# Later vectors with the seventh row block, turned rows of x one block later each

## The chip, the cores and the metric

The kernel runs on one core of a Trainium2 chip. The metric is the device time of one execution in microseconds (us); it is given as the median of several runs.

## The reference, cut to what matters

The program is one layer of a decoder trunk for 512 positions of 1024 channels, in float32: a mixer (an mLSTM head group beside a convolution group) and a causal ConvFFN, each behind a conditioned norm. The change touches only what feeds the first projection:

```python
cond = jax.nn.silu(c)
mod = cond @ ada_w[l] + ada_b[l]
sh1, sc1, g1, sh2, sc2, g2 = jnp.split(mod[:, None, :], N_MOD, axis=-1)
u = rms_norm(x, mix_pre_g[l]) * (1.0 + sc1) + sh1
proj = u @ w_in[l]
...
a, gt = jnp.split(glu, 2, axis=-1)
y = causal_dwconv(a * jax.nn.sigmoid(gt), cv_dw_w[l], cv_dw_b[l])
```

The two halves of `glu` are columns of `proj`, so they are products of `u` (512 x 1024) with columns of `w_in`. `c` is a vector, so a column of `sc1` or `sh1` is one dot product of `silu(c)` with a column of `ada_w`.

## The kernel before

The 1024 channels are 8 blocks of 128 rows (`KT` = 8, numbered k = 0 to 7), and 512 positions are the width of a tile. A tile is [128 partitions, 512]. The opening, up to line 375, makes the eight blocks of `u` one after the other and at once multiplies each with its weights into eight accumulators (`banks0`, the first four channel blocks of both halves of `glu`). So for each block k the opening needs:

- `w_glu0[k]`, the weights of that block for the eight accumulators: one transfer of 512 KB into a tile of the pool `adas`, which has two buffers (line 321).
- `adaT[k]`, the rows of `ada_w` for shift and scale of that block: two transfers of 512 KB into one tile of the pool `raws`, which also has two buffers (`first_load`, line 225). They are issued one block ahead.
- x, turned so that channels lie on the partitions. Blocks 0 to 3 are turned by TensorE from the untransposed x (`x_turn`); blocks 4 to 7 (`TURNED` = 4) come ready turned from memory, one transfer of 256 KB each into `xr[4]` to `xr[7]` (line 331).

VectorE sums the products of `adaT[k]` with `silu(c)` (`ada_sum`, line 276), which gives shift and scale (`gsk`, lines 334 and 335). Float32 products are made of three passes: each operand is split into a high and a low part, the high part by ScalarE (lines 170, 358, 361), the low part by VectorE (lines 171, 365, 367); `wk` are the split weights and `uh` and `ul` (in the code `hi`, `lo`) the split block of `u`. In blocks 4 to 7 line 354 first scales the turned rows by the norm's factor and the gain. TensorE's products are at line 316 in blocks 0 to 3 (all passes with the high part of `u` before those with the low part) and at lines 188 to 190 from block 4 on (three passes for one accumulator after the other, so that the second matmul of a block needs the low part).

All small vectors (gains, biases, convolution taps) lie side by side in one buffer `vec`. Its first 56 columns (`FIRST`; the bias of `ada_w` and the first gain) come early in a transfer of 28 KB on ScalarE's queue (line 229). The later 592 columns come in one transfer of 296 KB (line 328). Their first reader is `cvw` (line 408), which halves the 248 columns of taps of the 31-wide convolution; it is held on VectorE behind the last `ul` of the opening. The taps themselves (line 731) run on VectorE in the midst of everything up to the end of the attention heads; the short convolutions of the projections are line 462.

What sets the order: TensorE and SyncE run in the order of the source. SyncE issues nearly all transfers of the opening, and an issue that waits for a free buffer holds all that stand behind it. In the opening the other three engines keep the order of the source as well (`in_order`); behind it a planner orders them, by the dependencies and a simulated timeline.

```python
with tile.TileContext(nc, schedule_with_timeline_sim=True) as tc:
    with tc.manual_schedule(engines={mybir.EngineType.SP, mybir.EngineType.PE}):
```

In each block k from 1 on, SyncE thus issues: the weights of block k, the two transfers `adaT[k + 1]`, in block 1 the later vectors, and in blocks 1 to 4 one turned row block for use in block 4, 5, 6 or 7.

Of the kernel before, what the change touches and what calls it, by code (L numbers as in the profile page):

```python
# [52 lines left out]
def decoder_layer(ctx, tc, w_glu0, x, xT, c, adaT, vecs, w_glu, w_qko, w_v0, w_v, w_out, w_up, w_down, out):  # L53
# [75 lines left out]
    def vcol(name, i):  # L129
        a = VEC[name][0] + i  # L130
        return vec[:, a : a + 1]
# [32 lines left out]
    def w_split(src, name, pool=None, tag="w", eng=None):  # L164

        n = src.shape[1]
        pool = pool or wpool
        hi = pool.tile([P, T], F32R, tag=tag, name=f"{name}h")
        lo = pool.tile([P, T], F32R, tag=tag, name=f"{name}l")
        S.activation(hi[:, :n], src, AF.Copy)  # L170
        (eng or G).tensor_tensor(out=lo[:, :n], in0=src, in1=hi[:, :n].bitcast(F32), op=ALU.subtract)  # L171
        return hi, lo
# [8 lines left out]
    def blk(pieces, b):  # L181
        hi, lo = pieces[b // 4]
        a = (b % 4) * P
        return hi[:, a : a + P], lo[:, a : a + P]

    def mm3(ps, a, b, start, stop):

        PE.matmul(ps, a[0], b[0], start=start, stop=False)  # L188
        PE.matmul(ps, a[0], b[1], start=False, stop=False)  # L189
        PE.matmul(ps, a[1], b[0], start=False, stop=stop)  # L190
# [30 lines left out]
    def first_load(k):  # L221

        r = raws.tile([P, 2048], F32, tag="raw", name=f"ada{k}")
        for i in range(2):
            nc.sync.dma_start(r[:, i * D : (i + 1) * D], adaT[k][:, i * D : (i + 1) * D])
        first.append(r)
# [8 lines left out]
    TURNED = KT // 2  # L235
# [36 lines left out]
    def ada_sum(k, i):  # L272
        if i == 0:
            part[k] = small.tile([P, 2], F32, tag="adap", name=f"adap{k}")
        junk = small.tile([P, D], BF16, tag="junk", bufs=1, name=f"junk{k}_{i}")
        V.scalar_tensor_tensor(out=junk, in0=first[k][:, i * D : (i + 1) * D], scalar=1.0, in1=cb, op0=ALU.mult, op1=ALU.mult,
                               accum_out=part[k][:, i : i + 1])
# [6 lines left out]
    def x_out(j, eng):  # L284
        if eng is S:
            S.activation(xr[j], xT_ps[j], AF.Copy)
        else:
            V.tensor_copy(xr[j], xT_ps[j])
# [24 lines left out]
    def passes(wk, k, which):  # L313
        for a, b in ((0, 0), (1, 0), (0, 1)):
            for i in which:
                PE.matmul(banks0[i], blk(wk, i)[a], u[k][b], start=k == 0 and a == b, stop=False)

    for k in range(KT):
        wk = {}
        r = adas.tile([P, D], F32, tag="ada", name=f"wglu0_{k}")  # L320
        nc.sync.dma_start(r, w_glu0[k])
        if k == 0:
            w_hi = wpool.tile([P, T], F32R, tag="w", name="wglu0_0_1h")
            S.activation(w_hi, r[:, T:], AF.Copy)
        if k + 1 < KT:
            first_load(k + 1)
        if k == 1:
            nc.sync.dma_start(vec[:, FIRST:], vecs[:, FIRST:])
        if 1 <= k <= TURNED:
            j = TURNED + k - 1  # L330
            nc.sync.dma_start(xr[j], xT[j - TURNED])
        gsk = small.tile([P, 2], F32, tag="gsk", name=f"gsk{k}")
        gs, sh = gsk[:, :1], gsk[:, 1:]
        V.tensor_scalar(out=gs, in0=part[k][:, :1], scalar1=bp1[:, k : k + 1], scalar2=g32[:, k : k + 1], op0=ALU.add, op1=ALU.mult)
        V.tensor_scalar(out=sh, in0=part[k][:, 1:], scalar1=vcol("ada_b", 2 * k + 1), scalar2=None, op0=ALU.add)
        hi, lo = u[k]
        if k == 0:
            w_lo = wpool.tile([P, T], F32R, tag="w", name="wglu0_0_1l")
            V.tensor_tensor(out=w_lo, in0=r[:, T:], in1=w_hi.bitcast(F32), op=ALU.subtract)
            wk[1] = w_hi, w_lo  # L340
            S.activation(hi, xT_ps[0], AF.Identity, scale=gs, bias=sh)
            S.activation(rb, rb_ps, AF.Copy)
            V.tensor_scalar(out=xr[0], in0=xT_ps[0], scalar1=gs, scalar2=sh, op0=ALU.mult, op1=ALU.add)
            V.tensor_tensor(out=lo, in0=xr[0], in1=hi.bitcast(F32), op=ALU.subtract)
            wk[0] = w_split(r[:, :T], "wglu0_0_0", eng=V)
            for j in range(1, TURNED):
                x_out(j, S)
            for i in range(2):
                ada_sum(1, i)
            passes(wk, k, (6, 7, 4, 5))  # L350
            passes(wk, k, range(4))
            continue
        if k >= TURNED:
            V.scalar_tensor_tensor(out=xr[k], in0=xr[k], scalar=gs, in1=rb, op0=ALU.mult, op1=ALU.mult)
        for b in range(2):
            wk[b] = w_split(r[:, b * T : (b + 1) * T], f"wglu0_{k}_{b}", eng=V)
        if k < TURNED:
            S.activation(hi, xr[k], AF.Identity, scale=gs, bias=sh)
            S.activation(xr[k], xr[k], AF.Identity, scale=gs, bias=sh)
        else:  # L360
            S.activation(hi, xr[k], AF.Identity, bias=sh)
        if k + 1 < KT:
            ada_sum(k + 1, 0)
        if k < TURNED:
            V.tensor_tensor(out=lo, in0=xr[k], in1=hi.bitcast(F32), op=ALU.subtract)
        else:
            last_u = V.scalar_tensor_tensor(out=lo, in0=xr[k], scalar=sh, in1=hi.bitcast(F32), op0=ALU.add, op1=ALU.subtract)
        if k + 1 < KT:
            ada_sum(k + 1, 1)
        if k < 4:  # L370
            passes(wk, k, range(G0))
        else:
            for i, ps in enumerate(banks0):
                mm3(ps, blk(wk, i), u[k], False, k == KT - 1)
# [963 lines left out]
```

## Time and profile before

| What | Value |
| --- | --- |
| Median of three runs | 772.42 us (771.66 to 773.45) |
| The profiled execution's own time | 773.07 us |
| Its span | 771.4 us |
| TensorE (PE) busy, share of the span | 758.4 us, 98% |
| VectorE (DVE) busy | 610.1 us, 79% |
| ScalarE (ACT) busy | 403.8 us, 52% |
| GpSimd (POOL) busy | 352.2 us, 46% |
| Bytes read from and written to memory | 113.22 MB and 11.42 MB |

The profile is of one execution. Its span runs from the first instruction to the last one's end; the profiled execution's own time is 1.67 us longer. PE is TensorE's matmuls and PEld its weight loads, SP is SyncE; a q behind an engine's name (SPq) means that its sequencer issues something. A row of the timeline has the start in us from the span's start, the duration in us, the engine, the line of the kernel, the operation, output and inputs, how many instructions were merged, and in brackets the idle time of the engine before it and what ended it. A row of the chain of waits has start, length and the work or transfer on which the end hung.

### The profile page before, as it was taken

The page shows a single profiled execution, that of the slowest core. Times are in us where ns is not written, and L with a number is a line of the kernel's source. Part 1 is how long each engine was busy: PE and PEld are TensorE (multiplying, and loading weights), DVE is VectorE, ACT ScalarE, POOL GpSimd, SP SyncE. Part 2 cuts the span into 40 slices and gives each one's busy share as a digit, 9 for nine tenths or more (in the row PEclk, how much of TensorE's full clock was granted, in tenths as well). Part 3 has the DMA queues.
Part 4 walks back from the last instruction along what each step waited for, and adds up shares of the span by engine and source line. Part 5 has one row for each costly group of instructions (what it writes and reads, how often), then busy time and mean ns, then how long its engine had stood idle before and what let it go on. Part 6 is the DMA issues. An engine that isn't in the chain of part 4 may idle for free.

```text
span 771.4 us, 10631 instructions
## 1 busy us (share of the span) xinstructions
PE 758.4 (98%) x3709; PEld 637.5 (83%) x3709; DVE 610.1 (79%) x967; ACT 403.8 (52%) x761; POOL 352.2 (46%) x286
## 2 busy tenths in 40 slices
PE   7999999999999999999999999999999999999996
PEld 5788898778888888988888998888888888888885
DVE  6997999999999966756768798666556687799995
ACT  5447266776666447582253555444444444455762
POOL 2029578696798645443661456444444440000001
PEclk9999999999999999999999999999999999999998
DMA  8983214214022452434953753332233321777872
GB/s 320 377 301 132 90 55 164 82 40 151 30 84 107 153 179 105 164 110 164 366 199 126 253 197 130 130 130 88 110 117 129 130 89 62 255 271 241 298 260 109
DMA packets 36409, 125.33 MB, mean 162 GB/s; under 512 B 4194, under 2 KB 5634, under 8 KB 30468
## 3 DMA queue, kind: packets, MB, share of 16 engines
q1 hardware_dynamic: 24372, 96.17, 35.5%
q10 hardware_dynamic: 11984, 28.48, 10.6%
q8 instruction: 29, 0.48, 0.3%
q14 instruction: 24, 0.20, 0.1%
HBM read 113.22 MB, written 11.42 MB: 162 GB/s over the span
## 4 chain that ended last, share of the span: by engine, by line
PE 72%; DVE 21%; DMA 2%; ACT 2%; issue 2%; POOL 0%; ACTq 0%; DVEq 0%; POOLq 0%
PE up L189 10%; PE up L188 10%; DVE cv L731 10%; PE up L190 10%; PE p L1185 4%; PE glu L189 3%; PE glu L190 3%; PE glu L188 3%; PE p L189 3%; PE p L188 3%; PE p L190 3%; PE mixa L188 2%; PE mixa L190 2%; PE mixa L189 2%; PE mixb L189 2%; PE mixb L188 2%
## 5 line engine op out<-in xcount | busy, mean ns | idle before, releaser
L731 DVE SCALAR_TENSOR_TENSOR cv<-gt,cvw,cv 128x505 f32<-128x505 f32 (+24 forms) x200 | 137.3, 729 | 2.3 <-ACT cv L719 1.1
L685 POOL TENSOR_TENSOR ro2r<-ro2t,mhalf 128x1 f32<-128x1 f32 x1 | 0.5, 537 | 119.8 <-DVE ro2t L683 119.8
L727 POOL TENSOR_TENSOR cs<-cs,cs 128x510 f32<-128x510 f32 (+3 forms) x32 | 41.9, 1308 | 0.3
L171 POOL TENSOR_TENSOR wup_1024l<-wup,wup_1024h 128x512 fp32r<-128x512 f32 x20 | 27.4, 1372 | 31.6 <-ACT wup_1024h L170 31.6
L171 POOL TENSOR_TENSOR wup_0l<-wup,wup_0h 128x512 fp32r<-128x512 f32 x20 | 27.7, 1387 | 30.0 <-ACT wup_0h L170 30.0
L171 POOL TENSOR_TENSOR wup_1536l<-wup,wup_1536h 128x512 fp32r<-128x512 f32 x20 | 28.0, 1399 | 27.6 <-ACT wup_1536h L170 25.1
L155 DVE SCALAR_TENSOR_TENSOR junk<-ada,cb 128x1024 bf16<-128x1024 f32 x20 | 31.3, 1565 | 8.5 <-DMA ada<-in_adaT 8.4
L189 PE MATMUL up<-u2l,wup_0h 128*128 128x512 f32 (+1 forms) x100 | 36.5, 365 | 0.2 <-DVE u2l L910 0.2
L188 PE MATMUL up<-u2h,wup_0h 128*128 128x512 f32 (+1 forms) x100 | 36.5, 365 | 0.0
L188 PE MATMUL up<-u2h,wup_1024h 128*128 128x512 f32 (+1 forms) x100 | 36.4, 364 | 0.0
L190 PE MATMUL up<-u2h,wup_0l 128*128 128x512 f32 (+1 forms) x100 | 36.4, 364 | 0.0
L188 PE MATMUL up<-u2h,wup_512h 128*128 128x512 f32 (+1 forms) x100 | 36.4, 364 | 0.0
L189 PE MATMUL up<-u2l,wup_512h 128*128 128x512 f32 (+1 forms) x100 | 36.4, 364 | 0.0
L190 PE MATMUL up<-u2h,wup_512l 128*128 128x512 f32 (+1 forms) x100 | 36.4, 364 | 0.0
L188 PE MATMUL up<-u2h,wup_1536h 128*128 128x512 f32 (+1 forms) x100 | 36.4, 364 | 0.0
L189 PE MATMUL up<-u2l,wup_1536h 128*128 128x512 f32 (+1 forms) x100 | 36.4, 364 | 0.0
L190 PE MATMUL up<-u2h,wup_1536l 128*128 128x512 f32 (+1 forms) x100 | 36.4, 364 | 0.0
L190 PE MATMUL up<-u2h,wup_1024l 128*128 128x512 f32 (+1 forms) x100 | 36.4, 364 | 0.0
L189 PE MATMUL up<-u2l,wup_1024h 128*128 128x512 f32 (+1 forms) x100 | 36.3, 363 | 0.0
L171 POOL TENSOR_TENSOR wup_512l<-wup,wup_512h 128x512 fp32r<-128x512 f32 x20 | 27.7, 1383 | 14.0 <-ACT wup_512h L170 14.0
L725 ACT ACTIVATE cs<-gt,cvw 128x511 f32<-128x511 f32 (+4 forms) x40 | 27.4, 716 | 6.5 <-POOL cs L727 3.2
L170 ACT ACTIVATE wup_1024h<-wup 128x512 fp32r<-128x512 f32 x22 | 13.9, 631 | 25.1 <-PE up L189 20.4
(1072 smaller groups left out, 2667.0 us busy)
## 6 DMA issues: line engine op xcount, KB each, us to landing
wup<-in_w_up SPq DMA_DIRECT2D x22, 1024.0 KB, 6.5
wqko<-in_w_qko SPq DMA_DIRECT2D x12, 1024.0 KB, 4.8
ada<-in_adaT ACTq DMA_DIRECT2D x20, 512.0 KB, 4.6
ada<-in_adaT SPq DMA_DIRECT2D x16, 512.0 KB, 6.9
wo<-in_w_out SPq DMA_DIRECT2D x8, 1024.0 KB, 4.8
spare<-in_adaT ACTq DMA_DIRECT2D x12, 512.0 KB, 7.4
wd<-in_w_down SPq DMA_DIRECT2D x6, 768.0 KB, 6.7
g2kept<-g2d SPq DMA_DIRECT2D x11, 384.0 KB, 7.3
```

The costliest lines, as they stand in the source:

```text
L155: t = V.scalar_tensor_tensor(out=junk, in0=r, scalar=1.0, in1=cb, op0=ALU.mult, op1=ALU.mult, accum_out=mod[:, i : i + 1])
L170: S.activation(hi[:, :n], src, AF.Copy)
L171: (eng or G).tensor_tensor(out=lo[:, :n], in0=src, in1=hi[:, :n].bitcast(F32), op=ALU.subtract)
L188: PE.matmul(ps, a[0], b[0], start=start, stop=False)
L189: PE.matmul(ps, a[0], b[1], start=False, stop=False)
L190: PE.matmul(ps, a[1], b[0], start=False, stop=stop)
L685: G.tensor_tensor(out=r, in0=t, in1=mhalf[:, :1], op=ALU.pow)
L725: S.activation(t[:, d:], cvx[j][:, : T - d], AF.Copy, scale=w(CK - 1 - d))
L727: G.tensor_tensor(out=side[:, d:], in0=side[:, d:], in1=t[:, d:], op=ALU.add)
L731: last_tap[0] = V.scalar_tensor_tensor(out=cp[:, d:], in0=cvx[j][:, : T - d], scalar=w(CK - 1 - d), in1=cp[:, d:], op0=ALU.mult, op1=ALU.add)
L1185: PE.matmul(ps[q], x, y, start=False, stop=m == NM - 1 and i == 2, skip_group_check=True)
```

## The change

The transfer of the later vectors is issued in block 6 instead of block 1, in the same place within the block (behind the two transfers `adaT[k + 1]`). The four turned row blocks are issued in blocks 2 to 5 instead of 1 to 4. The order of SyncE's issues, block by block:

| Block | Before | After |
| --- | --- | --- |
| 1 | w 1, ada 2, vectors, x 4 | w 1, ada 2 |
| 2 | w 2, ada 3, x 5 | w 2, ada 3, x 4 |
| 3 | w 3, ada 4, x 6 | w 3, ada 4, x 5 |
| 4 | w 4, ada 5, x 7 | w 4, ada 5, x 6 |
| 5 | w 5, ada 6 | w 5, ada 6, x 7 |
| 6 | w 6, ada 7 | w 6, ada 7, vectors |
| 7 | w 7 | w 7 |

```diff
         if k + 1 < KT:
             first_load(k + 1)
-        if k == 1:
+        if k == 6:
             nc.sync.dma_start(vec[:, FIRST:], vecs[:, FIRST:])
-        if 1 <= k <= TURNED:
-            j = TURNED + k - 1
+        if 2 <= k <= TURNED + 1:
+            j = TURNED + k - 2
             nc.sync.dma_start(xr[j], xT[j - TURNED])
```

## The prediction

> **What bounds the kernel now.** I read the page first, then the stages of the opening, then the chain of waits, the timeline and the transfers issued by SyncE.
>
> ```profile
> span 771.4 us, 10631 instructions
> PE 758.4 (98%) x3709; PEld 637.5 (83%) x3709; DVE 610.1 (79%) x967; ACT 403.8 (52%) x761; POOL 352.2 (46%) x286
> PE 72%; DVE 21%; DMA 2%; ACT 2%; issue 2%; POOL 0%; ACTq 0%; DVEq 0%; POOLq 0%
> L731 DVE SCALAR_TENSOR_TENSOR cv<-gt,cvw,cv 128x505 f32<-128x505 f32 (+24 forms) x200 | 137.3, 729 | 2.3 <-ACT cv L719 1.1
> ```
>
> TensorE is busy for 98% of the span, so the whole kernel holds only 13.0 us in which it is idle, and DMA is 2% of the chain that ended last. A change of transfers can pay only where a transfer holds TensorE up. The stages show where transfers are dense (columns: busy time of PE, PEld, DVE, ACT and POOL with instruction counts, granted clock, share of the DMA engines, GB/s):
>
> ```profile
> 10.00:20.00 10.00, 9.10 (x50) 8.16 (x50) 8.49 (x18) 5.01 (x11) 1.27 (x2) 1.00 1.01 379
> 20.00:30.00 10.00, 9.95 (x44) 7.94 (x43) 9.40 (x22) 4.50 (x7) 0.00 (x0) 1.00 0.99 375
> 30.00:40.00 10.00, 9.71 (x44) 7.70 (x43) 9.53 (x19) 5.38 (x9) 0.00 (x0) 1.00 1.02 387
> 40.00:50.00 10.00, 10.00 (x46) 8.29 (x45) 10.00 (x20) 3.89 (x7) 0.00 (x0) 1.00 0.90 310
> 120.00:180.00 60.00, 60.00 (x272) 48.34 (x271) 59.65 (x97) 40.39 (x74) 46.10 (x37) 1.00 0.30 105
> ```
>
> From 10 to 40 us the DMA engines are full, at 375 to 387 GB/s; every transfer there delays those queued behind it. TensorE nevertheless runs nearly without a break, at full granted clock. Later, from 120 to 180 us, VectorE is the full engine (59.65 of 60 us). The chain of waits, in order of time, names the one place where the two meet:
>
> ```profile
> 21.83 7.96 DMA wglu<-in_w_glu
> 29.81 0.64 ACT wglu_0h L170
> 30.47 0.69 DVE wglu_0l L171
> 37.97 0.68 DVE ul L367
> 38.70 0.50 PE glu L189
> 116.86 1.28 ACT L574
> ```
>
> The weights of the fourth row block (k = 3), issued at 21.83, land 7.96 us later; ScalarE splits them, VectorE continues, and through VectorE's work of blocks 3 and 4 the chain reaches a matmul at 38.70 us. From there it is TensorE alone, one matmul after the other, up to 116.86 us. So time won at 38.70 is kept at least that far.
>
> ```profile
> 20.39 0.20 DVE L335 TENSOR_SCALAR gsk<-adap,vec 128x1 f32<-128x1 f32 x1
> 29.20 0.20 DVE L335 TENSOR_SCALAR gsk<-adap,vec 128x1 f32<-128x1 f32 x1
> 29.81 0.63 ACT L170 ACTIVATE wglu_0h<-wglu 128x512 fp32r<-128x512 f32 x1 [2.86 <-DMA wglu<-in_w_glu]
> 30.47 0.69 DVE L171 TENSOR_TENSOR wglu_0l<-wglu,wglu_0h 128x512 fp32r<-128x512 f32 x1 [1.07 <-ACT wglu_0h L170]
> 37.90 0.74 DVE L367 SCALAR_TENSOR_TENSOR ul<-xr,gsk,uh 128x512 fp32r<-128x512 f32 x1
> 38.01 0.39 PE L188 MATMUL glu<-uh,wglu_0h 128*128 128x512 f32 x1
> 38.70 0.50 PE L189 MATMUL glu<-ul,wglu_0h 128*128 128x512 f32 x1 [0.29 <-DVE ul L367]
> 39.27 0.39 PE L188 MATMUL glu<-uh,wglu_0h 128*128 128x512 f32 x1
> 43.02 0.75 DVE L367 SCALAR_TENSOR_TENSOR ul<-xr,gsk,uh 128x512 fp32r<-128x512 f32 x1
> 44.04 0.39 PE L188 MATMUL glu<-uh,wglu_0h 128*128 128x512 f32 x1
> ```
>
> VectorE ends its small work for block 3 at 29.40 and stands for 1.07 us, since ScalarE got the weights only at 29.81. In block 4 the first matmul starts at 38.01, the second needs `ul`, which is done at 38.64 (37.90 + 0.74). The stall is larger than the 0.29 us marked as idle. Matmuls 4 (39.27) and 25 (44.04, the first of block 5) are 21 apart, so one takes (44.04 - 39.27) / 21 = 0.227 us; unstalled, matmul 25 would start at 38.01 + 24 x 0.227 = 43.46. It starts 0.58 us later. That is the stall's price.
>
> **The change part by part.**
>
> ```profile
> 15.40 0.43 SPq L328 DMA_DIRECT2D vec<-in_vecs  x1
> 15.87 0.43 SPq L331 DMA_DIRECT2D xr<-in_xT  x1
> 17.91 0.33 SPq L321 DMA_DIRECT2D wglu<-in_w_glu  x1
> 21.18 0.43 SPq L331 DMA_DIRECT2D xr<-in_xT  x1
> 21.83 0.33 SPq L321 DMA_DIRECT2D wglu<-in_w_glu  x1
> 29.98 0.42 SPq L331 DMA_DIRECT2D xr<-in_xT  x1
> 39.81 0.81 SPq L225 DMA_DIRECT2D ada<-in_adaT  x2
> 41.99 0.33 SPq L321 DMA_DIRECT2D wglu<-in_w_glu  x1
> xr<-in_xT SPq DMA_DIRECT2D x4, 256.0 KB, 7.4
> vec<-in_vecs SPq DMA_DIRECT2D x1, 296.0 KB, 6.9
> L354 DVE SCALAR_TENSOR_TENSOR xr<-xr,gsk,rb_s x4: 745/747/750, 34.9 to 50.3; 128x512 f32<-128x512 f32 x4
> L408 DVE TENSOR_SCALAR cvw<-vec x1: 1380/1380/1380, 52.8 to 52.8; 128x248 f32<-128x248 f32 x1
> ```
>
> No instruction and no byte is added or removed; five issues of 0.42 or 0.43 us change places on SyncE's queue. SyncE is not the limit: before 17.91 it has been idle since 16.30, since it waits for a buffer that VectorE frees, so the issues it loses or gains cost nothing.
>
> *Vectors out of block 1, turned rows one block later.* Before, the vectors and the first two turned rows stand ahead of the weights issued at 21.83; after, one turned row does, at about 21.2 us. That is 296 + 256 = 552 KB less ahead, 565,248 bytes, at 375 GB/s 1.51 us. The queue does not run dry meanwhile: time to landing is about 7 us against the 1.51 us taken out. So these weights land near 28.3 us, ScalarE's split ends near 28.9, before VectorE asks for it at 29.40, and the whole 1.07 us goes. The weights issued at 17.91 also land earlier, but VectorE never waited for them. Bounds of this term: 0 (the landing does not move) and 1.07 us (VectorE does not wait, and has its next work queued). I take 1.07, as 1.51 is above it.
>
> *What this gives TensorE.* `ul` of block 4 is then done at 38.64 - 1.07 = 37.57; the second matmul wants it at 38.01 + 0.23 = 38.24. The stall goes entirely, already if VectorE gains 0.40 to 0.46 of the 1.07. What is late next is nothing in the opening: block 5's `ul`, done at 43.77, comes at 42.70, and its second matmul then wants it at 43.46 + 0.23 = 43.69. TensorE's work, not VectorE's, limits from here, so 0.58 us is the gain and the rest of the 1.07 stays idle time of VectorE. Without the chain over TensorE up to 116.86 none of it would be kept.
>
> *The turned rows' own users.* The first is now issued with the second's old place, near 21.2; by 7.4 us it lands near 28.6. It is read at 34.9 (first start of line 354), or 33.8 after the gain: 5.2 us of cover. The last moves from 29.98 to the next block; two blocks lie between 29.98 and 40.62, the end of the pair issued at 39.81, so one is some 5 us and it is issued near 35, lands near 42.7 and is read at 50.3, or 49.2 after the gain: 6.5 us of cover. Cost 0; it would cost what it is late beyond the cover.
>
> *The vectors in block 6.* They follow the pair issued at 39.81 and stand ahead of the weights issued at 41.99. The first reader of the later columns is `cvw` at 52.8 (51.7 after the gain). Issued between 39.6 (40.62 - 1.07) and 40.7 and 6.9 us long, they land by 47.6: 4.1 us of cover. Behind them the last block's weights have the same bytes ahead as before in sum, and the DMA share there is 0.90. Cost 0. The earlier columns of the same buffer are read each block; the read at 20.39 came while the transfer of 15.40 was still under way (it landed at 22.3), so these reads do not wait for the later columns, wherever that transfer stands.
>
> The sum is -0.58 us. Against the profiled execution, 773.07 us (its span of 771.4 and 1.67 around it), that is 772.5; the median of the three times shown, 772.42, lies 0.65 below that execution, so the forecast is 772.42 - 0.58 = 771.8 us. This is 0.08%, below the 0.2% (1.54 us) that a measurement of this kernel can tell from no change.
>
> **Rivals.**
>
> *The order behind the opening changes for the worse.* TensorE's and SyncE's order is written by hand, and VectorE's, ScalarE's and GpSimd's inside the opening too; behind it a planner orders those three by a simulated timeline, in which it prices SyncE's transfers as well. It moves instructions far:
>
> ```profile
> 1.28 0.48 DVE L594 MEMSET Ms<- 128x512 f32 x1
> ```
>
> Line 594 stands far behind the opening in the source and runs at 1.28 us. If the opening's simulated time shifts, ties between the taps of line 731 and work on which TensorE waits may fall the other way. The place is the stretch of full VectorE behind 116.86 us; the price is 0.729 us a tap (page, first group). Three taps net ahead of TensorE's inputs cost 2.19 us, less 0.58 makes +1.61: 774.0 us; four make 774.8. It decides from three taps on; below that the result is within 0.2%. For it: the taps fill VectorE wherever there is room, so many ties exist. Against it: the whole later timeline shifts together, and the taps have no input from the moved transfers before `cvw`.
>
> *The order changes for the better.* The same mechanism with the other sign: two taps give -0.58 - 1.46 = 770.4 us, three 769.6.
>
> *Nothing moves.* The landing of the weights is set by something other than the bytes ahead, and the 0.58 us stays: 772.4 us. Against it stands the DMA share of 0.99 and landing times of 7 us.
>
> *Late landing.* The transfers moved behind others come after their users: the vectors decide from 11 us to landing on (52.8 - 1.07 - 40.7 = 11.0), against 6.9 measured. Each microsecond more holds VectorE, with all that is queued behind `cvw`, as long; 3 us more would give at most 772.4 + 3 - 0.6 = 774.8. [...] The trace says that the early place was taken from transfers needed sooner, and that 4.1 us of cover stay.
>
> **How the numbers follow.** Forecast 0.40 (771.8); nothing moves 0.08 (772.4); order worse 0.24, of which 0.22 from three taps on; order better 0.26; late landing 0.02. Faster by over 0.2% (below 770.9): 0.26. Slower (above 774.0): 0.22 + 0.02 = 0.24. Within: 0.50. I give the planner's two cases half, since neither sign can be read from a trace of before. The range reaches to three taps on the good side and four on the bad, 769.5 to 774.8; the forecast's own range, from the bounds of its one term, is 771.8 to 772.4.
>
> **What would show it.** Right: the second matmul of block 4 follows the first by 0.23 us; VectorE's 1.07 us before the split of block 3 is gone; the weights of block 3 land about 6.4 us after issue; `cvw` and line 354 wait for no transfer; behind the opening all engines have the same order, 0.58 us earlier. Wrong: a matmul of the opening waiting for a turned row or for `ul`; a transfer named as releaser of `cvw`; or other counts of taps between the projections' convolutions (line 462), which would show the planner at work.

## The result, and the profile after

The changed kernel takes **777.1 us** (median; 775.89 to 778.98) against 772.93 (771.66 to 773.95) for the kernel before in the same session: ratio 1.0056, 95% interval [1.0037, 1.0076]. It is 4.2 us slower, and 2.3 us above the upper end of my range. The profiled execution took 777.78 us. Its page, lines in the order of those shown of before:

```profile
span 776.1 us, 10635 instructions
PE 759.8 (98%) x3709; PEld 638.4 (82%) x3709; DVE 615.6 (79%) x967; ACT 402.9 (52%) x761; POOL 353.2 (46%) x286
PE 71%; DVE 17%; DMA 5%; ACT 4%; issue 2%; POOL 0%; ACTq 0%; SPq 0%; DVEq 0%; POOLq 0%
```

VectorE has the same 967 instructions and is busy 5.5 us longer (615.6 against 610.1): some of them take longer. The opening, in the timeline of the changed kernel:

```profile
21.61 0.94 SPq L321 DMA_DIRECT2D wglu<-in_w_glu  x1
28.79 0.63 ACT L170 ACTIVATE wglu_0h<-wglu 128x512 fp32r<-128x512 f32 x1 [2.31 <-DMA wglu<-in_w_glu]
29.46 0.69 DVE L171 TENSOR_TENSOR wglu_0l<-wglu,wglu_0h 128x512 fp32r<-128x512 f32 x1 [0.27 <-ACT wglu_0h L170]
37.80 0.39 PE L188 MATMUL glu<-uh,wglu_0h 128*128 128x512 f32 x1
38.02 0.39 PE L189 MATMUL glu<-ul,wglu_0h 128*128 128x512 f32 x1
39.75 0.42 SPq L328 DMA_DIRECT2D vec<-in_vecs  x1
51.88 1.38 DVE L408 TENSOR_SCALAR cvw<-vec 128x248 f32<-128x248 f32 x1
```

ScalarE starts on block 3's weights 7.18 us after the issue instead of 7.98, VectorE stands 0.27 us instead of 1.07, and the second matmul follows the first by 0.22: the stall is gone, and `cvw` waits for no transfer. From there up to 202 us TensorE is 0.80 us ahead of before: 0.21 us of it stood already in front of the stall (the first matmul of block 4 starts at 37.80 instead of 38.01), the other 0.59 are the stall. Then it is lost, at two places. TensorE's waits, first of before, then of the changed kernel (in total, times, longest):

```profile
PE s L514 <- DVE E L515: 0.4, 1, 0.4
PE hT L555 <- DVE hn L549: 0.4, 1, 0.4
PE s L514 <- DVE so L557: 0.3, 1, 0.3
```

```profile
PE s L514 <- DVE so L557: 4.4, 2, 2.4
PE gT L653 <- DVE gains L863: 0.8, 1, 0.8
```

The s matmuls (line 514) of heads 1 and 2 wait until VectorE has made `so`, the gated output of the head before (line 557). `so` is made from hT, TensorE's transposes of `hn` (line 555). Start of the same matmul in both traces:

| Matmul | Before | After | Lag of after |
| --- | --- | --- | --- |
| hT, line 555, head 0 | 203.28 | 201.55 | -1.73 |
| s, behind a wait of 2.00 | 206.76 | 207.20 | +0.44 |
| s, behind a wait of 2.36 | 261.34 | 263.92 | +2.58 |
| seventh s after it | 264.13 | 268.34 | +4.21 |
| gT, line 653, behind a wait of 0.80 | 392.71 | 397.25 | +4.54 |

At hT the lag is larger than 0.80 because before's transposes wait for `hn`, which VectorE ends at 203.22. From 2.58 to 4.21 there is no wait: these matmuls run slower. The stages of the changed kernel (granted clock third from the end):

```profile
264.00:266.00 2.00, 2.00 (x4) 0.93 (x5) 1.74 (x2) 2.00 (x5) 2.00 (x3) 0.76 0.69 209
266.00:268.00 2.00, 2.00 (x4) 0.97 (x3) 2.00 (x3) 0.95 (x3) 2.00 (x2) 0.50 0.24 72
268.00:270.00 2.00, 2.00 (x8) 1.34 (x8) 2.00 (x2) 0.00 (x0) 2.00 (x2) 0.89 0.84 246
```

Shortly behind the wait of 2.36 us TensorE is granted half its clock for 3.41 us (265.04 to 268.45), and loses 1.63 us more.

**Why `so` is late.** The planner has made another order behind the opening. VectorE around `so` of head 0 with GpSimd beside `hn`, before and then after:

```profile
196.34 5.84 DVE L731 SCALAR_TENSOR_TENSOR cv<-gt,cvw,cv 128x502 f32<-128x502 f32 x9
202.09 1.13 DVE L549 TENSOR_SCALAR hn<-hn,fac 128x256 f32<-128x256 f32 x4
204.41 0.68 DVE L557 SCALAR_TENSOR_TENSOR so<-so,hT 128x512 f32<-128x512 f32 x1
199.72 1.03 POOL L546 TENSOR_TENSOR fac<-ssq,mhalf 128x4 f32<-128x4 f32 x1
205.39 1.30 POOL L171 TENSOR_TENSOR wqko_1024l<-wqko,wqko_1024h 128x512 fp32r<-128x512 f32 x1 [4.63 <-PE v L189]
```

```profile
193.37 4.26 DVE L549 TENSOR_SCALAR hn<-hn,fac 128x256 f32<-128x256 f32 x4
206.47 0.68 DVE L557 SCALAR_TENSOR_TENSOR so<-so,hT 128x512 f32<-128x512 f32 x1
193.49 1.39 POOL L171 TENSOR_TENSOR wqko_0l<-wqko,wqko_0h 128x512 fp32r<-128x512 f32 x1
194.83 1.34 POOL L727 TENSOR_TENSOR cs<-cs,cs 128x509 f32<-128x509 f32 x1
196.14 1.34 POOL L749 TENSOR_TENSOR ysq<-ysq,ydl 128x512 f32<-128x512 f32 x1
```

The four `hn` (line 549, the head's output times its norm factor) stand ahead of eleven taps instead of behind nine, and take 4.26 us instead of 1.13. One by one (least, median, longest in ns), before and after:

```profile
L549 DVE TENSOR_SCALAR hn<-hn,fac x4: 346/346/347, 202.1 to 202.9; 128x256 f32<-128x256 f32 x4
```

```profile
L549 DVE TENSOR_SCALAR hn<-hn,fac x4: 344/1381/1394, 193.4 to 196.2; 128x256 f32<-128x256 f32 x4
```

In before GpSimd stands still from 200.75 to 205.39; here it works without a break, and three of four `hn` last until just after its running instruction ends (0.15 us later each time). From the last convolution of line 462 to `so` VectorE had 22 taps and 19.01 us before (185.40 to 204.41), and 21 taps and 21.82 us after (184.65 to 206.47): one tap fewer, 2.81 us more. With some 0.65 us for the missing tap, the same work took about 3.5 us longer. Three collisions at 1.04 us are 3.1 of that; line 543 takes 0.60 us more as well, line 745 0.15 less.

### The profile page after: what moved, and what is told of

The parts are those of the page before. It is cut to its first block, busy times and chain, and to the rows that moved or that the text cites. A ratio compares the mean times of both kernels' runs of the same rounds, so it can differ in the third digit from the quotient of the medians.

```text
span 776.1 us, 10635 instructions
## 1 busy us (share of the span) xinstructions
PE 759.8 (98%) x3709; PEld 638.4 (82%) x3709; DVE 615.6 (79%) x967; ACT 402.9 (52%) x761; POOL 353.2 (46%) x286
## 4 chain that ended last, share of the span: by engine, by line
PE 71%; DVE 17%; DMA 5%; ACT 4%; issue 2%; POOL 0%; ACTq 0%; SPq 0%; DVEq 0%; POOLq 0%
PE up L189 10%; PE up L188 10%; PE up L190 10%; DVE cv L731 9%; PE p L1185 4%; PE glu L189 3%; PE glu L190 3%; PE glu L188 3%; PE p L189 3%; PE p L188 3%; PE p L190 3%; PE glu L316 2%; DMA spare<-in_adaT 2%; DMA x<-in_x 2%; PE qko L188 1%
## 5 line engine op out<-in xcount | busy, mean ns | idle before, releaser
L731 DVE SCALAR_TENSOR_TENSOR cv<-gt,cvw,cv 128x502 f32<-128x502 f32 (+24 forms) x200 | 137.3, 729 | 3.2 <-ACT cv L719 2.1
```

The source lines that it names most:

```text
L731: last_tap[0] = V.scalar_tensor_tensor(out=cp[:, d:], in0=cvx[j][:, : T - d], scalar=w(CK - 1 - d), in1=cp[:, d:], op0=ALU.mult, op1=ALU.add)
```

## Experiments

**Theory**: the transfers themselves cost nothing; the new order puts `hn` beside GpSimd's work, the collisions make `so` late, and TensorE pays the wait and sometimes a stretch of half clock. **Rivals**: the moved transfers disturb something later; or the order is bad for another reason (taps ahead of `so`).

To part order from transfers, a kernel is planned once with the transfers of one version, and each engine's order is then given to the kernel under test as order-only dependencies (the kernels so pinned to before's order, e1 and e11, took 1.0005 and 0.9994 of before's time):

```diff
+ order = build(layout, BEFORE)[2]            # places on VectorE, ScalarE, GpSimd
...
+ for a, b in zip(places, places[1:]):
+     tc.add_manual_dep(mine[e][b], mine[e][a].name, DependencyInfo(NoSync, DATA))
```

**e1 (the changed transfers in before's order) and e2 (before's transfers in the changed kernel's order).**

> The moved transfers with VectorE's, ScalarE's and GpSimd's instructions in the order of the kernel before. Theory A, the planner's new order costs the time: the stall of 0.58 us in block 4 of the opening goes as in the changed kernel and no new wait appears behind it, so 0.6 us below before, ratio 0.9992 (0.9980 to 1.0000). Theory B, the moved transfers themselves cost (late landing, other transfers pushed back): as slow as the changed kernel, some 4 us above before, ratio 1.005.

> The transfers of the kernel before with the three engines' instructions in the order of the changed kernel. Theory A: slow without any moved transfer; the changed kernel's 4.2 us plus the 0.6 us that the opening does not win here, so 4.5 to 5.2 us above before, ratio 1.006 to 1.007. Theory B: as before, ratio 1.000.

Measured: e1 1.0005 [0.9994, 1.0016], e2 1.0084 [1.0071, 1.0097]. The order alone brings the loss, the transfers alone do not. Both times lie above what was expected. What the transfers gain in the opening does not show in e1's time; its profiled execution, for one, lost 1.6 us to half clock from 16.92 us on. e2 is some 2 us slower than the changed kernel, though its three engines have the same order; the two intervals just overlap, and what the difference is stays open.

**e3 (before, with the changed order only from 185 to 213 us) and e4 (after, with before's order there).**

```diff
+ order, other = build(layout, BEFORE)[2], build(layout, AFTER)[2]
+ for e, (a, b) in zip(ENGINES, ((284, 326), (187, 211), (94, 107))):
+     order[e][a:b] = other[e][a:b]
```

> The transfers of before and the order of before, except for one stretch taken from the changed kernel's order: the end of the first attention head and start of the next (185 to 213 us), where the normalised head output (line 549) stands before nine taps instead of behind them and ScalarE and GpSimd differ with it. Theory A1, this one stretch starts the loss and what follows (the wait at 261 us, the lower clock, the wait at 393 us) are its sequels: 3.5 to 5 us above before, ratio 1.005 to 1.006. Theory A2, the loss is spread over the fifty or so small swaps: less than half, ratio 1.000 to 1.002.

> The changed kernel with the same stretch (185 to 213 us) in the order of before, all else in its own order. Theory A1: the loss goes, 0.5 us below before or level, ratio 0.999 to 1.001. Theory A2: more than half of the loss stays, ratio 1.003 to 1.005.

Measured: e3 1.0060 [1.0046, 1.0073]. These few instructions suffice. Timeline and stages of e3:

```profile
209.25 2.07 PE L514 MATMUL s<-q_0c,k_2c 128*128 128x512 f32 x2 [2.00 <-DVE so L557]
208.00:210.00 2.00, 0.75 (x1) 0.50 (x2) 2.00 (x4) 0.77 (x2) 0.00 (x0) 0.82 0.00 0
210.00:212.00 2.00, 2.00 (x4) 0.70 (x3) 2.00 (x4) 2.00 (x5) 1.45 (x2) 0.50 0.00 0
```

e4, 1.0047 [1.0035, 1.0059], was not repaired, and its ratio is the one expected if the loss were spread over many swaps: the stretch is sufficient, not necessary. Its `hn` take 0.35 us again, but the order ahead of the stretch, still the changed one, delays VectorE by a wait for GpSimd, and `hn` comes late instead (timeline and waits of e4); half clock follows there too, 0.50 in one stretch:

```profile
189.36 1.77 DVE L745 SCALAR_TENSOR_TENSOR ydl<-ysum,gt 128x512 f32<-128x512 f32 x1 [1.47 <-POOL gt L739]
PE hT L555 <- DVE hn L549: 2.4, 1, 2.4
```

**e5, e6 and the control e11: the collision taken away.** Only head 0's four `hn` go to ScalarE; every other instruction keeps its place. e5 is e3 so edited, e6 the changed kernel, e11 the kernel before.

```diff
- V.tensor_scalar(out=hv, in0=hv, scalar1=fac[:, tt : tt + 1], scalar2=None, op0=ALU.mult)
+ S.activation(hv, hv, AF.Copy, scale=fac[:, tt : tt + 1])      # h == 0
```

> The kernel of before with the changed kernel's order in the stretch 185 to 213 us (as in e3, 1.0060), and in it the four hn multiplications of head 0 (line 549) run on ScalarE as activations with the same scale; nothing else changes its place on any engine. Theory of collisions (VectorE's hn waits for GpSimd's instruction that runs beside it, 1.38 us where 0.35 would do): VectorE is rid of the 4.24 us that the four took in e3, is 2 to 4 us earlier at so (line 557), PE's wait of 2.00 us ahead of the s matmuls at 207 goes and with it the stretch of half clock behind it (1.8 us): 773.0 to 774.5 us, ratio 1.000 to 1.002. Rival (the taps of the short convolution put ahead of so are what makes it late, hn is no part of it, or ScalarE is now the late one): the wait stays at 1.5 us or more and the ratio at 1.005 to 1.006.

> The changed kernel with its own order on every engine, and the four hn multiplications of head 0 on ScalarE instead of VectorE. Theory of collisions: VectorE is 4.4 us earlier behind 198 us; the first wait for so (2.00 us at 206.8) goes, and what is carried to the second one (2.36 us at 261, with its half clock) falls by as much as VectorE has not filled up meanwhile: 773 to 774.5 us, ratio 1.000 to 1.002. If only the first wait goes and the second is caused by the order of head 1 itself: 775 us, ratio 1.003. Rival (hn is no part of the loss): 777.1 us, ratio 1.0056.

> Control: the kernel of before with its own order and transfers, only the four hn of head 0 on ScalarE instead of VectorE. In before they take 0.35 us each, since GpSimd stands still there, so VectorE is rid of 1.4 us that cost no more than the waits of 0.4 and 0.3 us behind them. Theory of collisions: no change to a small gain, ratio 0.9985 to 1.0005; so the 4 us that e6 gained against the changed kernel came from the collisions and not from hn's work itself. Rival (taking hn's work off VectorE is worth as much anywhere): ratio 0.995 to 0.996.

Measured: e5 0.9990 [0.9977, 1.0003], e6 0.9994 [0.9979, 1.0009], e11 0.9994 [0.9981, 1.0008]. The same edit takes away e3's 0.6% and the changed kernel's 0.56%, and 0.06% where nothing collides: the loss goes with the slow `hn`, while taking `hn`'s own work off VectorE gains next to nothing in before. In e6 VectorE is rid of 4.5 us at `hn`, 3.1 us of collisions and 1.4 us of its own work. What the 1.4 us are worth where VectorE is late is not shown apart, but the 3.1 us alone are more than the first wait of 2.00. VectorE, the waits and the page's busy times of e6:

```profile
197.71 7.11 DVE L731 SCALAR_TENSOR_TENSOR cv<-gt,cvw,cv 128x503 f32<-128x503 f32 x11
204.74 0.67 DVE L557 SCALAR_TENSOR_TENSOR so<-so,hT 128x512 f32<-128x512 f32 x1
PE s L514 <- DVE so L557: 1.5, 1, 1.5
PE 757.7 (98%) x3709; PEld 637.2 (83%) x3709; DVE 609.4 (79%) x963; ACT 404.4 (52%) x765; POOL 352.9 (46%) x286
```

The eleven taps still stand ahead of `so` and take the same 7.11 us, so they were not the cause. One wait of 1.5 us is left of 4.4, at head 2, and VectorE is busy 6.2 us less for 1.4 us of work given away.

**e7: what the half clock costs.** e3, with the wait filled by matmuls that nobody uses.

```diff
+ for _ in range(9): PE.matmul(fill, u[0][0][:, :P], u[0][0], start=True, stop=True)   # head 1, ahead of s
```

> e3 (before with the changed kernel's order from 185 to 213 us) and nine more matmuls of 0.227 us (2.04 us, their result is not used) into a free bank of PSUM in front of head 1's s matmuls, where PE stood 2.00 us in e3. Theory that the idle time itself lowers the granted clock: the wait is filled, the s matmuls run at full clock behind it, and 1.8 us of e3's 4.2 us are saved: ratio 1.0037 (1.0025 to 1.0048), granted clock 0.95 or more in every stretch of 2 us from 206 to 214. Rival (the half clock comes from something else that falls there, or costs nothing since VectorE is the late one anyway): ratio as e3, 1.0060 (1.005 to 1.007).

Measured: 1.0040 [1.0027, 1.0054], against e3's 1.0060 [1.0046, 1.0073]. Timeline and stages of e7:

```profile
206.22 2.23 PE L506 MATMUL fill<-uh 128*128 128x512 f32 x9
208.28 1.02 PE L514 MATMUL s<-q_0c,k_2c 128*128 128x512 f32 x2
208.00:210.00 2.00, 2.00 (x7) 0.96 (x6) 2.00 (x4) 2.00 (x4) 1.05 (x1) 1.00 0.00 0
210.00:212.00 2.00, 2.00 (x9) 1.34 (x8) 2.00 (x4) 2.00 (x6) 2.00 (x3) 1.00 0.35 92
```

Two s matmuls take 1.02 us instead of e3's 2.07, at a clock of 1.00. One execution does not show that the idle time is what lowers the clock, since not every such wait did; the last section has what the other traces add. The time agrees with some 1.5 us, but e3 and e7 were timed in different sessions and their intervals overlap, so the price rests on the traces.

**e8 and e9: each half of the change alone, the planner free.** (e8's expectation gives the vectors 540 KB of the 552; it is 296, and 256 for the row block.)

```diff
- if k == 1:                       # e8: vectors in block 6, rows as before
+ if k == 6:
...
- if 1 <= k <= TURNED:             # e9: rows one block later, vectors as before
+ if 2 <= k <= TURNED + 1:
```

> Half of the change alone: the later vectors go with the seventh row block, the turned rows of x stay where they were; the planner makes its own order. Theory that the planner's order, whichever of the two moves sets it off, makes the loss: here it puts the instructions between 185 and 213 us as in the changed kernel, so two waits of 2 us for so and a ratio of 1.0056 (1.004 to 1.008). Rival (the turned rows are what does it; the vectors alone are harmless): 1.000 (0.999 to 1.001). In the opening the vectors are 540 KB of the 552 KB that leave the queue, so the stall at 38.70 us should be gone as in the changed kernel.

> The other half of the change alone: the turned rows of x come one block later each, the later vectors stay with the second block; the planner makes its own order. Theory that either half sets off the same new order: it puts the instructions of head 0 as in the changed kernel, so four hn of which three take 1.38 us, two waits for so of 2 us or more, ratio 1.0055 (1.004 to 1.008). Rival (the vectors alone make the planner turn): ratio 1.000 (0.9985 to 1.0015). In the opening 256 KB less stand ahead of block 3's weights, 0.7 us at 375 GB/s, so VectorE's wait ahead of their split is about half of that of before (0.4 us).

Measured: e8 1.0040 [1.0026, 1.0055], e9 1.0052 [1.0035, 1.0069]. `hn` and the waits, of e8 and of e9:

```profile
L549 DVE TENSOR_SCALAR hn<-hn,fac x4: 341/1380/1393, 194.1 to 197.0; 128x256 f32<-128x256 f32 x4
PE s L514 <- DVE so L557: 4.4, 2, 2.4
```

```profile
L549 DVE TENSOR_SCALAR hn<-hn,fac x4: 343/1380/1384, 193.2 to 196.1; 128x256 f32<-128x256 f32 x4
PE s L514 <- DVE so L557: 4.4, 2, 2.4
```

Either half sets off the same order: behind the opening VectorE, ScalarE and GpSimd run the changed kernel's instructions in the changed kernel's order in both traces. So here it took neither of the two moves in particular.

**e10 and e12: the changed transfers without the loss.** e10 is e5, e12 is e11, each with the changed transfers.

> The changed kernel's transfers with the order of e5 (before's order, in it the changed kernel's stretch 185 to 213 us, the four hn of head 0 on ScalarE). Theory: the gain of the opening (0.5 us on the mean of the profiled runs so far) and that of e5 (0.0010 of the time) add up: 772.3 us, ratio 0.9985 (0.997 to 1.000). Rival (the gain of the opening is taken up again by VectorE, which is just in time behind it): ratio as e5, 0.999 to 1.000.

> The changed kernel's transfers, before's order, and the four hn of head 0 on ScalarE. Theory: e1 (1.0005) less what e11 gains over before, and without the stall of the opening: ratio 0.9985 to 1.000. Rival (hn on ScalarE is late for the transposes of line 555, since ScalarE comes to it only behind its own queue): a wait of PE for hn of 0.5 us or more at 203 and a ratio over 1.0005.

Measured: e10 0.9999 [0.9988, 1.0010], e12 0.9992 [0.9982, 1.0003]. No version is shown to beat before. In e12 TensorE stood 1.0 us for `ul` in the opening, although the 552 KB were gone from ahead of block 3's weights.

## Why the prediction was wrong, step by step

- **Opening.** In the profiled execution the stall of 0.58 us went, and the 0.59 us won were kept up to 202. Two rows came short of the forecast: ScalarE began on the weights of block 3 7.18 us after their issue, not about 6.4, so they came 0.80 us sooner and not 1.51, and VectorE still stood 0.27 us. It was enough, since the stall needs only some 0.4 us. The step that failed in this term is that I read it off one execution. TensorE's wait for block 4's `ul` was 0.29, 1.02, 1.01, 0, 0.86 and 0 us in six profiled executions with before's transfers (before, e2, e3, e5, e7, e11), 0.53 on the mean; and 0, 0, 0, 0.85, 0.47 and 1.02 with the changed ones (after, e1, e4, e6, e10, e12), 0.39. With the same transfers ScalarE began on block 3's weights at 27.70 (e1) and at 30.60 (e12), a scatter of 2.9 us against the 1.51 us that I worked out for the bytes. The waits' means differ by 0.14 us, and e1 shows no gain. What scatters the landing is open.
- **Turned rows, vectors, late landing.** Right: line 354 and `cvw` waited for no transfer; `vec` was issued at 39.75, inside the 39.6 to 40.7 given.
- **The planner.** This is where the forecast failed. The likeliest case, the same order 0.6 us earlier, did not come; the rival that I gave 0.24 did, in the full VectorE stretch behind 116.86 us where I put it. The argument against it, that the whole timeline shifts together, failed. Its sign came true without its mechanism: no tap was added ahead of `so`.
- **Its price.** This term made the range too short: its worst case was 774.8, 2.3 us below the time measured. I priced a changed order by taps, 0.729 us each, up to four, as if every instruction lasted as long in another order; the taps ahead of `so` fell by one. What the runs showed instead is 3 x 1.04 us of collisions at `hn`, paid by TensorE as waits of 2.00 and 2.36 us, and 1.63 us of half clock. The table's sum: from -1.73 to +0.44 and +2.58 by the waits, +4.21 by the clock.
- **What would show it.** The sign named, other counts of taps between line 462's convolutions, is there but small (one tap at a time; up to `so` 22 and 21); it would not have led to the cause. Busy time of VectorE at an equal number of instructions did.

## What to carry to other kernels

When a planner orders part of a kernel, an edit ahead of that part can change its order as well (here the edit and each of its halves gave the same new one); to know what the edit itself is worth, measure it once with the old order pinned. Compare busy time at equal instruction counts first: where it rises, look for an instruction that lasts as long as another engine's, and move it to an engine on which it does not (here `hn`: 1.38 us on VectorE beside GpSimd's 1.34 to 1.39, 0.50 on ScalarE in e6). A gain read off one execution's wait on a transfer needs the same wait in several executions before it counts.

## What was not expected of the hardware

- VectorE's 128x256 `tensor_scalar` from SBUF to SBUF (`hn`) takes 0.35 us in before, where GpSimd stands still, and 1.38 us in three of four in after, beside GpSimd's work; line 745, with two inputs in SBUF, takes between 0.68 and 1.76 us in before. The taps of line 731, whose running sum `cv` lies in PSUM, keep 0.71 to 0.75 us in both traces. What makes `hn` wait and the taps not, no run here shows.
- The granted clock fell to 0.50 for some 3.4 us (3.41 in after) behind or at the end of single waits of 2.00 (e3), 2.13 (e1, in the opening), 2.36 to 2.37 (after, e2, e8) and 2.44 us (e4), and cost 1.6 us in e1, 1.63 in after and 1.79 in e3 (the s matmuls up to the next projection, against e7); with waits of 1.99 (e2), 2.00 (after, in front of 207.20; e8; e9) and 2.38 us (e9) it stayed at 1.00.
- What parts these waits is where they lie, as far as the traces show it. In after the granted clock changes at 265.04, 268.45 and 773.63, whole multiples of 3.413 us apart: the fall at the kernel's end comes 505.18 us behind the rise, 148 times 3.413. Cut along this grid from 12.46 us on, the interval that ends with the fall at 265.04 holds 2.29 us in which TensorE is idle. The wait of 2.00 in front of 207.20 is cut at 207.02; its interval holds 1.82, and every other one with TensorE at work at most 1.04. In before, cut back from its only fall at 767.19, the interval ahead of that fall holds 2.30 us, every other one with TensorE at work from 12.84 us on at most 0.90. In e1 the wait of 2.13 lies almost whole in the 3.41 us ahead of the fall at 16.92, which hold 1.93 us idle. Two rows of after, then two of e1 (TensorE's busy time is the second number of a row, the granted clock the third from the end):

```profile
203.60:207.02 3.42, 1.60 (x14) 1.40 (x12) 3.42 (x6) 0.26 (x1) 1.63 (x2) 1.00 0.00 0
261.63:265.04 3.41, 1.12 (x3) 0.65 (x4) 3.01 (x5) 2.01 (x5) 3.41 (x3) 1.00 0.52 190
13.50:16.92 3.42, 1.49 (x6) 1.24 (x7) 3.10 (x8) 2.95 (x6) 0.00 (x0) 1.00 1.03 419
16.92:20.33 3.41, 3.41 (x10) 2.63 (x9) 3.38 (x9) 1.96 (x4) 0.00 (x0) 0.50 1.02 402
```

The other falls are placed here from the mean clock of stretches of 2 us (0.82 in 208 to 210 puts e3's at 209.28), so what follows is an estimate to some 0.03 us. In e3 the wait of 2.00, from 207.25 to 209.25, lies whole in the 3.41 us ahead of its fall. Counted back in steps of 3.413 from the falls at 266.20 (e2) and 264.84 (e8), the grid cuts the waits that cost nothing, e2's 1.99 (207.62 to 209.61) at 208.17 and e8's 2.00 (some 206.0 to 208.0) at 206.81. Where the grid lies in e9, and so why its 2.38 us cost nothing, is not shown. The wait that e7 filled (206.22 to 208.28) would have left some 2.06 us idle (an estimate from these times), more than the 1.93 that was enough in e1, if it lay in one interval, which is not shown either. The falls at 265.04 (after) and 209.28 (e3) are 16.3 intervals apart: the grid lies differently from execution to execution, and about the same wait, 2.00 us for head 0's `so`, cost the half clock in e3 and not in after.
